# A hybrid encoder block on one core: x loaded before the first modulation's weights, scaled on ScalarE and GpSimd, with idle products on TensorE

## The chip, the cores and the metric

One core of a Trainium2 chip runs the whole kernel in one launch. The metric is device time in microseconds (us) of one execution, lower is better; three executions of the kernel before are shown, with their median. The engines are named as in the profile: PE is TensorE, DVE is VectorE, ACT is ScalarE, POOL is GpSimd, SP is the queue that issues most transfers.

## The reference

One encoder layer on 512 tokens of width 1024. Only its head is touched by the change:

```python
c_act = silu(c)
mod = c_act @ w_ada + b_ada
shift1, scale1, gate1, shift2, scale2, gate2 = split(mod, 6)
h = rmsnorm(x, g_norm1) * (1 + scale1) + shift1
z = h @ w_in
y_attn = mla_group(z[:, :448], ...)
y_sg = sgu_group(z[:, 448:], ...)
x = x + gate1 * (concat(rmsnorm(y_attn), rmsnorm(y_sg)) @ w_o)
h2 = rmsnorm(x, g_norm2) * (1 + scale2) + shift2
out = rmsnorm(x + gate2 * peer(h2), g_final)
```

`w_ada` is 1024 x 6144 in float32, so each of the six modulation vectors needs 4 MB of weights. The rest (latent attention, the gating group, the 16384 experts of `peer`) is the same before and after.

## The kernel before, in words

**The modulation vectors.** A vector of `mod` is made without TensorE doing the reduction over rows: the weights of group g come as eight tiles of 128 x 1024 (`mod_load`, L128), and VectorE adds them up, each scaled by its column of `silu(c)`, in one 128 x 1024 accumulator `macc` (`mod_group`, L138: one scaling, six fused multiply-adds, and the last one in two halves). Then eight 128 x 128 transposes on TensorE and two sums on VectorE turn the accumulator into columns (`mod_cols`, L153). There is one accumulator buffer for all groups (`tag="macc"`, L139): the next group's first write waits until the last reader of this group's sum is done. Groups 1 (scale1) and 0 (shift1) are made first, their 16 tiles loaded on SP's queue into a pool of 12 buffers; groups 2 to 5 follow later, loaded on GpSimd's queue into three buffers, behind a small copy called `mark` (L247, L373).

**The first normalization.** `normed_T` (L191) squares and sums the four 128 x 1024 blocks of x on ScalarE (L183), takes the power -1/2 on GpSimd (L114), scales x on VectorE (L197), transposes it on TensorE (L201), applies scale1 and shift1 (`affine`, L185: even columns j on VectorE, odd ones on ScalarE), and splits the result into a high and a low float32r part (`split_into`, L76: a cast on ScalarE, a subtraction on VectorE), the tiles hT.

**What follows.** `load_w` (L208) loads and splits w_in; the first product with it gives the latents `lat` and the rope key `krp` (L304 to L315). Meanwhile VectorE makes the rope angles `ang` (L272 to L281) and adds up group 2. The latents are squared, normalized (L320 to L327) and transposed (`trl`, L331); the rope key is rotated (`rope_from`, L288, with `kr_sw` on TensorE, `kr_t` and `kr` on VectorE); then the queries `qr` and `qn`, the keys `kn` and the values `v` are multiplied (L333 to L351), and the `vp` projection with `wv` follows (L372). `kr_sw` and the three `trl` share two PSUM buffers (L125).

**What sets the order.** Each engine works through its own queue in order. A scheduler sets that order when the program is built, so a change in one part can move instructions of others; SP's and GpSimd's transfers are issued in order too. From 100 us on the program is TensorE's: attention, the output projection, the routing, and the dense and gathered experts.

Lines 237 to 249 set the head:

```python
ws1 = [mod_load(1, c) for c in range(KD)]
...
    nc.sync.dma_start(t, a["x"][b * P:(b + 1) * P, :])
...
ws0 = [mod_load(0, c) for c in range(KD)]
s1 = mod_scale(1, g1c, ws1)
sh1 = mod_cols(0, ws0)
mark = nc.gpsimd.tensor_copy(mark, sh1[:, 0:1])
...
normed_T(xs, s1, sh1, hT[0], hT[1], "n1")
```

Of the kernel before, what the change touches and what calls it, by code (L numbers as in the profile page):

```python
# [9 lines left out]
F32 = mybir.dt.float32  # L10
# [5 lines left out]
ALU = mybir.AluOpType  # L16
# [41 lines left out]
def tile_kernel(ctx: ExitStack, tc: tile.TileContext, a: dict, out: bass.AP):  # L58
# [59 lines left out]
    with ExitStack() as fr:  # L118
# [34 lines left out]
        def mod_cols(g, ws=None):  # L153
            acc = mod_group(g, ws)
            m = cp.tile([P, KD], F32, name=f"mcolb{g}")
            for hf in range(2):
                p = ps.tile([P, 512], F32, name=f"mcol{g}_{hf}", tag="oacc" if ws and hf else "mod", bufs=1)
                for j in range(4):
                    nc.tensor.transpose(p[:, j * P:(j + 1) * P],  # L159
                                        acc[:, (hf * 4 + j) * P:(hf * 4 + j + 1) * P], ident)  # L160
                nc.vector.reduce_sum(m[:, hf * 4:hf * 4 + 4], p.rearrange("p (j k) -> p j k", k=P), axis=AX.X)
            nc.vector.tensor_add(m, m, bada[:, g * KD:(g + 1) * KD])
            return m

# [15 lines left out]
        def sumsq(src, dst, name):  # L180
            w = src.shape[-1]
            sq = B.tile([P, D], BF16, name=name, tag="sq", bufs=1)
            nc.scalar.activation(sq[:, :w], src, AF.Square, accum_out=dst)  # L183
# [4 lines left out]
            else:  # L188
                nc.vector.tensor_scalar(t, p, scol[:, j:j + 1], shcol[:, j:j + 1], op0=ALU.mult, op1=ALU.add)

        def normed_T(src, scol, shcol, dhi, dlo, tag, post=None):  # L191
            ss = cp.tile([P, NB], F32, name=f"ss_{tag}")
            for b in range(NB):
                sumsq(src[b], ss[:, b:b + 1], f"sq_{tag}{b}")
            r = rstd_of(ss, D, tag)
            for b in range(NB):
                nc.vector.tensor_scalar_mul(src[b], src[b], r[:, b:b + 1])  # L197
            for j in range(KD):
                p = (tr_ps if j % 3 == 2 else acc_ps)(f"trx_{tag}{j}")
                for b in range(NB):  # L200
                    nc.tensor.transpose(p[:, b * P:(b + 1) * P], src[b][:, j * P:(j + 1) * P], ident)  # L201
                t = B.tile([P, T], F32, name=f"nt_{tag}{j}", tag="nt", bufs=2)
                affine(j, t, p, scol, shcol)
                split_into(dhi[:, j, :], dlo[:, j, :], t)
                if post is not None:
                    post(j, t)

        def load_w(name, src, c0, w):  # L208
            res = []
            for kh in range(2):  # L210
                raw = B.tile([P, 4, 512], F32, name=f"{name}{kh}r", tag="wr", bufs=2)
# [2 lines left out]
                    src[kh * 512:(kh + 1) * 512, c0:c0 + w].rearrange("(c p) n -> p c n", p=P))  # L214
                hi = B.tile([P, 4, 512], F32R, name=f"{name}{kh}h", tag="wh", bufs=2)
                lo = B.tile([P, 4, 512], F32R, name=f"{name}{kh}l", tag="wl", bufs=2)
                split_into(hi[:, :, :w], lo[:, :, :w], raw[:, :, :w])
                res.append((hi, lo))
            return res

# [13 lines left out]

        m0_st = ExitStack()
        M0 = pool(m0_st, "M0", side="right")
        ws1 = [mod_load(1, c) for c in range(KD)]
        xs = []
        for b in range(NB):
            t = B.tile([P, D], F32, name=f"x{b}", tag=f"y{b}")  # L240
            nc.sync.dma_start(t, a["x"][b * P:(b + 1) * P, :])
            xs.append(t)
        ws0 = [mod_load(0, c) for c in range(KD)]
        s1 = mod_scale(1, g1c, ws1)
        sh1 = mod_cols(0, ws0)
        mark = cp.tile([P, 1], F32, name="mark")
        mark = nc.gpsimd.tensor_copy(mark, sh1[:, 0:1])  # L247
        hT = [B.tile([P, KD, T], F32R, name=f"hT{i}", tag=f"hT{i}") for i in range(2)]
        normed_T(xs, s1, sh1, hT[0], hT[1], "n1")

        m0_st.close()
        qkv_st = ExitStack()
# [7 lines left out]
        with ExitStack() as s1st:  # L260
# [35 lines left out]
                nc.vector.tensor_add(o, o, t)  # L296


            wl = load_w("wl", a["w_in"], 0, 512)
            nc.sync.dma_start(wuq, a["w_uq"].rearrange("(c p) n -> p c n", p=P))  # L300
            nc.sync.dma_start(wukv, a["w_ukv"])
            pss = [acc_ps(f"lat{b}") for b in range(NB)]
# [712 lines left out]
```

## Time and profile before

| what | value |
|---|---|
| three executions | 1567.84, 1566.68, 1567.22 us, median 1567.22 us |
| the profiled execution | 1570.06 us, of which its span is 1568.3 us |
| PE busy | 1492.6 us, 95% of the span |
| DVE busy | 1240.9 us, 79% |
| ACT busy | 636.6 us, 41% |
| POOL busy | 397.1 us, 25% |

The profile is of one execution, with the start and end of every instruction. "Idle before" is the time that an engine stood still before an instruction, with the one that ended the wait. A float32 product that is no transpose stands in the trace as two entries. The granted clock is TensorE's: 1.00 is 2.4 GHz and 0.50 is 1.2 GHz. The profiled execution took 2.84 us more than the median of the three.

### The profile page before, as it was taken

How to read it: one execution, taken by the hardware profiler on the slowest of the kernel's cores; microseconds unless marked ns; L12 is line 12 of the kernel's file. 1: busy time of each engine (PE TensorE's matmuls, PEld its weight loads, DVE VectorE, ACT ScalarE, POOL GpSimd, SP SyncE). 2: the span in 40 equal slices, each digit the busy share in tenths (PEclk: the TensorE clock that was granted, in tenths of full speed). 3: DMA queues.
4: the chain of work that ended last, by engine and by line, in shares of the span. 5: the costliest groups of instructions: out<-in, count | busy, mean ns of one | idle time of the engine just before them, and what ended most of it. 6: DMA issues, size and time to landing. Idle time of an engine off the chain costs nothing.

```text
span 1568.3 us, 21451 instructions
## 1 busy us (share of the span) xinstructions
PE 1492.6 (95%) x7675; PEld 1317.9 (84%) x7675; DVE 1240.9 (79%) x2388; ACT 636.6 (41%) x1092; POOL 397.1 (25%) x335
## 2 busy tenths in 40 slices
PE   2899999998979999999999999999999999999996
PEld 1765787887879999999999999999999999998884
DVE  6937865579989997987887878878888888886774
ACT  2533434432338997334333333333333333332343
POOL 1202100000000000002554444444544544542210
PEclk9899999999999999999999999999999999999998
DMA  9626334331325769666999999988999998987873
GB/s 366 232 79 223 130 132 148 112 104 48 101 94 159 237 211 300 218 224 220 354 351 319 321 330 328 326 318 318 336 330 314 326 325 315 333 287 230 256 237 121
DMA packets 147226, 380.71 MB, mean 243 GB/s; under 512 B 11184, under 2 KB 59840, under 8 KB 146864
## 3 DMA queue, kind: packets, MB, share of 16 engines
q1 hardware_dynamic: 103472, 221.02, 40.5%
q0 software_dynamic: 42352, 153.62, 28.7%
q10 hardware_dynamic: 1296, 4.72, 0.8%
q8 instruction: 60, 0.98, 0.2%
q14 instruction: 46, 0.38, 0.1%
HBM read 349.16 MB, written 30.15 MB: 242 GB/s over the span
## 4 chain that ended last, share of the span: by engine, by line
PE 86%; DVE 7%; DMA 3%; ACT 1%; issue 1%; POOL 0%; SPq 0%; ACTq 0%; POOLq 0%; DVEq 0%
PE out L83 11%; PE out L84 11%; PE out L82 11%; PE pa L82 11%; PE pa L84 11%; PE pa L83 11%; PE gg L770 5%; DMA wada<-w_ada 2%; PE q L82 1%; PE q L84 1%; PE q L83 1%; PE yo L82 1%; PE yo L84 1%; PE yo L83 1%; DVE macc L149 1%
## 5 line engine op out<-in xcount | busy, mean ns | idle before, releaser
L842 POOL DMA_INDIRECT gu<-peer_u,idx x128 | 181.3, 1417 | 653.6 <-DVE w17l L78 467.6
L842 POOL DMA_INDIRECT gv<-peer_v,idx x128 | 173.0, 1351 | 235.0 <-DVE accg L862 209.0
L850 DVE SCALAR_TENSOR_TENSOR scr<-gu,h2g 128x1024 bf16<-128x1024 f32 x128 | 156.5, 1222 | 24.1 <-DMA gu<-peer_u,idx 21.8
L862 DVE SCALAR_TENSOR_TENSOR accg<-gv,wg,accg 128x1024 f32<-128x1024 f32 x127 | 162.8, 1282 | 7.1 <-DMA gv<-peer_v,idx 4.6
L770 PE MATMUL gg<-o,o 128*128 128x128 f32 x768 | 96.0, 280 | 3.6 <-ACT o L764 2.0
L770 PEld LDWEIGHTS gg<-o,o 128*128 128x128 f32 x768 | 94.6, 196 | 4.1 <-ACT o L764 4.1
L908 DVE TENSOR_TENSOR a<-a,g 128x384 f32<-128x384 f32 x128 | 69.1, 550 | 6.4 <-DMA g<-gd 2.9
L764 ACT ACTIVATE o<-o1b,gT 128x128 f32<-128x128 bf16 x192 | 63.4, 405 | 13.8 <-DVE o1b L751 7.2
L518 ACT ACTIVATE a<-pa 128x384 f32<-128x384 f32 x128 | 61.7, 483 | 13.2 <-PE pa L84 13.2
L149 DVE SCALAR_TENSOR_TENSOR macc<-wada,csil,macc 128x1024 f32<-128x1024 f32 x40 | 51.2, 1280 | 9.5 <-DMA wada<-w_ada 9.1
L753 DVE TENSOR_TENSOR o<-iota_s,gT 128x1024 f32<-128x1024 f32 x48 | 58.4, 1216 | 0.3 <-PE gg L770 0.2
L757 DVE TENSOR_SCALAR o<-iota_s,gT 128x128 f32<-128x128 f32 x192 | 53.2, 339 | 0.0
L779 ACT COPY st<-gg 128x512 f32<-128x512 f32 x96 | 50.5, 581 | 0.0
L159 PE MATMUL mcol<-ident_s,macc 128*128 128x128 f32 x32 | 7.4, 391 | 26.6 <-DVE macc L146 23.1
L135 POOL DMA_DIRECT2D wada<-w_ada x32 | 17.1, 535 | 59.9 <-DVE macc L149 24.3
L159 PEld LDWEIGHTS mcol<-ident_s,macc 128*128 128x128 f32 x32 | 5.5, 201 | 28.3 <-DVE macc L146 17.9
L424 ACT ACTIVATE pe<-s,mx 128x512 f32<-128x512 f32 x16 | 11.0, 688 | 28.4 <-DVE mx L422 20.8
L684 PE MATMUL sc<-keys_s,qT 128*128 128x128 f32 x128 | 18.1, 284 | 2.8 <-ACT qT L681 2.8
L751 DVE TENSOR_TENSOR o1b<-erep,gB 128x512 bf16<-128x512 bf16 x48 | 20.0, 416 | 0.9 <-ACT gB L734 0.9
L684 PEld LDWEIGHTS sc<-keys_s,qT 128*128 128x128 f32 x128 | 15.6, 191 | 5.7 <-ACT qT L681 4.3
L531 DVE MAX8 v12d<-s 128x8 f32<-128x128 f32 x48 | 12.7, 280 | 9.4 <-ACT s L686 9.4
L431 PEld LDWEIGHTS o<-vv,pts 128*128 128x128 f32 x128 | 16.1, 192 | 2.3 <-DVE mx L422 0.8
(2789 smaller groups left out, 4952.2 us busy)
## 6 DMA issues: line engine op xcount, KB each, us to landing
gd<-st SPq DMA_DIRECT2D x12, 1984.0 KB, 7.9
g<-gd SPq DMA_DIRECT2D x31, 768.0 KB, 8.4
wada<-w_ada POOLq DMA_DIRECT2D x32, 512.0 KB, 4.7
wada<-w_ada SPq DMA_DIRECT2D x16, 512.0 KB, 10.1
x<-x SPq DMA_DIRECT2D x4, 512.0 KB, 12.4
x<-x ACTq DMA_DIRECT2D x4, 512.0 KB, 3.8
x2d<-x ACTq DMA_DIRECT2D x4, 512.0 KB, 2.8
gu<-peer_u,idx POOLq DMA_INDIRECT x128, 7.3
```

Of the source, the lines that this page charges most:

```text
L82: nc.tensor.matmul(o, lhsT=lh, rhs=rh, start=first, stop=False)
L83: nc.tensor.matmul(o, lhsT=lh, rhs=rl, start=False, stop=False)
L84: nc.tensor.matmul(o, lhsT=ll, rhs=rh, start=False, stop=last)
L149: nc.vector.scalar_tensor_tensor(acc, w, csil[:, c:c + 1], acc, op0=ALU.mult, op1=ALU.add)
L518: nc.scalar.activation(t, p[:, :TD], AF.Gelu)
L753: nc.vector.tensor_tensor(o2s[n], iota.unsqueeze(1).to_broadcast([P, UT, P]), tT[:, 1, t0:t0 + UT].unsqueeze(2).to_broadcast([P, UT, P]), ...
L764: nc.scalar.activation(o1s[n][:, i, :], e[:, :, i], AF.Copy, scale=tT[:, 2, t0 + i:t0 + i + 1])
L770: nc.tensor.matmul(pgs[n][i // 4][:, i % 4 * P:(i % 4 + 1) * P], lhsT=o2[:, i, :], rhs=o1[:, i, :], start=True, stop=True)
L842: nc.gpsimd.indirect_dma_start(out=g, out_offset=None, in_=src, in_offset=bass.IndirectOffsetOnAxis(ap=idx[:, s:s + 1], axis=0))
L850: nc.vector.scalar_tensor_tensor(scr, g, 1.0, st["h2g"], op0=ALU.mult, op1=ALU.mult, accum_out=actg[:, n:n + 1])
L862: nc.vector.scalar_tensor_tensor(accg, g, wg[:, s:s + 1], accg, op0=ALU.mult, op1=ALU.add)
L908: nc.vector.tensor_tensor(wv3, wv3, gt[:, :, e % GE, :], op=ALU.mult)
```

## The change

x's four tiles are loaded ahead of the 16 modulation tiles. Each block of x gets its own sum of squares; GpSimd does the multiply-add and the power, ScalarE the scaling, all of it ahead of the two modulation sums in the program's text, so VectorE's queue holds no scaling of x any more. After the transposes of group 1 come 24 products of the identity with the first 128 columns of the accumulator, into a PSUM buffer that nothing reads. `mark`, behind which groups 2 to 5 are loaded, now waits for the low part of column 5 of hT instead of for shift1. The split of the second half of the first w_in block is put behind the low part of column 1. `normed_T` is called from one place, so its unused `post` goes.

```diff
--- before.py
+++ after.py
@@ -159,6 +159,10 @@
                     nc.tensor.transpose(p[:, j * P:(j + 1) * P],
                                         acc[:, (hf * 4 + j) * P:(hf * 4 + j + 1) * P], ident)
                 nc.vector.reduce_sum(m[:, hf * 4:hf * 4 + 4], p.rearrange("p (j k) -> p j k", k=P), axis=AX.X)
+            if ws and g:
+                p = acc_ps("warm")
+                for k in range(24):
+                    nc.tensor.matmul(p[:, :P], lhsT=ident, rhs=acc[:, :P], start=True, stop=True)
             nc.vector.tensor_add(m, m, bada[:, g * KD:(g + 1) * KD])
             return m
 
@@ -188,13 +192,8 @@
             else:
                 nc.vector.tensor_scalar(t, p, scol[:, j:j + 1], shcol[:, j:j + 1], op0=ALU.mult, op1=ALU.add)
 
-        def normed_T(src, scol, shcol, dhi, dlo, tag, post=None):
-            ss = cp.tile([P, NB], F32, name=f"ss_{tag}")
-            for b in range(NB):
-                sumsq(src[b], ss[:, b:b + 1], f"sq_{tag}{b}")
-            r = rstd_of(ss, D, tag)
-            for b in range(NB):
-                nc.vector.tensor_scalar_mul(src[b], src[b], r[:, b:b + 1])
+        def normed_T(src, scol, shcol, dhi, dlo, tag):
+            los = []
             for j in range(KD):
                 p = (tr_ps if j % 3 == 2 else acc_ps)(f"trx_{tag}{j}")
                 for b in range(NB):
@@ -202,10 +201,10 @@
                 t = B.tile([P, T], F32, name=f"nt_{tag}{j}", tag="nt", bufs=2)
                 affine(j, t, p, scol, shcol)
                 split_into(dhi[:, j, :], dlo[:, j, :], t)
-                if post is not None:
-                    post(j, t)
-
-        def load_w(name, src, c0, w):
+                los.append(last_lo[0])
+            return los
+
+        def load_w(name, src, c0, w, after=None):
             res = []
             for kh in range(2):
                 raw = B.tile([P, 4, 512], F32, name=f"{name}{kh}r", tag="wr", bufs=2)
@@ -214,7 +213,10 @@
                     src[kh * 512:(kh + 1) * 512, c0:c0 + w].rearrange("(c p) n -> p c n", p=P))
                 hi = B.tile([P, 4, 512], F32R, name=f"{name}{kh}h", tag="wh", bufs=2)
                 lo = B.tile([P, 4, 512], F32R, name=f"{name}{kh}l", tag="wl", bufs=2)
-                split_into(hi[:, :, :w], lo[:, :, :w], raw[:, :, :w])
+                with ExitStack() as order:
+                    if after and kh:
+                        order.enter_context(tc.issue_after(after.ins))
+                    split_into(hi[:, :, :w], lo[:, :, :w], raw[:, :, :w])
                 res.append((hi, lo))
             return res
 
@@ -234,19 +236,25 @@
 
         m0_st = ExitStack()
         M0 = pool(m0_st, "M0", side="right")
-        ws1 = [mod_load(1, c) for c in range(KD)]
         xs = []
         for b in range(NB):
             t = B.tile([P, D], F32, name=f"x{b}", tag=f"y{b}")
             nc.sync.dma_start(t, a["x"][b * P:(b + 1) * P, :])
             xs.append(t)
+        ws1 = [mod_load(1, c) for c in range(KD)]
         ws0 = [mod_load(0, c) for c in range(KD)]
+        for b in range(NB):
+            ss = cp.tile([P, 1], F32, name=f"ss_n{b}")
+            sumsq(xs[b], ss, f"sq_n{b}")
+            nc.gpsimd.tensor_scalar(ss, ss, 1.0 / D, EPS, op0=ALU.mult, op1=ALU.add)
+            nc.gpsimd.tensor_tensor(ss, ss, nhalf[:, :1], op=ALU.pow)
+            nc.scalar.activation(xs[b], xs[b], AF.Copy, scale=ss)
         s1 = mod_scale(1, g1c, ws1)
         sh1 = mod_cols(0, ws0)
+        hT = [B.tile([P, KD, T], F32R, name=f"hT{i}", tag=f"hT{i}") for i in range(2)]
+        los = normed_T(xs, s1, sh1, hT[0], hT[1], "n1")
         mark = cp.tile([P, 1], F32, name="mark")
-        mark = nc.gpsimd.tensor_copy(mark, sh1[:, 0:1])
-        hT = [B.tile([P, KD, T], F32R, name=f"hT{i}", tag=f"hT{i}") for i in range(2)]
-        normed_T(xs, s1, sh1, hT[0], hT[1], "n1")
+        mark = nc.gpsimd.tensor_copy(mark, hT[1][:, 5, 0:1].bitcast(F32))
 
         m0_st.close()
         qkv_st = ExitStack()
@@ -296,7 +304,7 @@
                 nc.vector.tensor_add(o, o, t)
 
 
-            wl = load_w("wl", a["w_in"], 0, 512)
+            wl = load_w("wl", a["w_in"], 0, 512, los[1])
             nc.sync.dma_start(wuq, a["w_uq"].rearrange("(c p) n -> p c n", p=P))
             nc.sync.dma_start(wukv, a["w_ukv"])
             pss = [acc_ps(f"lat{b}") for b in range(NB)]
```

The scheduler's order changes in these places. Ahead of the latents, VectorE's queue (macc is the accumulator, wada a weight tile, x a block of x, n_r the power). Before, with what each row waits for:

```order
L167 SCALAR_TENSOR_TENSOR mcolb_150<-mcolb_150,g1c 128x8 [waits DMASW3_49,DVE_49]
L112 TENSOR_SCALAR n_ms<-ss_n_193 128x4 [waits Activation_49]
L197 TENSOR_SCALAR x_116<-x_116,n_r 128x1024 [waits DMAHW1_49,Pool_49]
L143 TENSOR_SCALAR macc_165<-wada_0_124,csil 128x1024 [waits DMAHW5_49]
L197 TENSOR_SCALAR x_118<-x_118,n_r 128x1024 [waits DMAHW2_49]
L149 SCALAR_TENSOR_TENSOR macc_165<-wada_1_126,csil,macc_165 128x1024 [waits DMAHW6_49,DVE_49]
```

And with the change, from the same place to the end of the second sum:

```order
L171 SCALAR_TENSOR_TENSOR mcolb_174<-mcolb_174,g1c 128x8 [waits DMASW3_49,DVE_49]
L143 TENSOR_SCALAR macc_214<-wada_0_124,csil 128x1024 [waits DMAHW5_49,PE_49]
L149 SCALAR_TENSOR_TENSOR macc_214<-wada_1_126,csil,macc_214 128x1024 [waits DMAHW6_49,DVE_49]
L149 SCALAR_TENSOR_TENSOR macc_214<-wada_2_128,csil,macc_214 128x1024 [waits DMAHW7_49,DVE_49]
L149 SCALAR_TENSOR_TENSOR macc_214<-wada_3_130,csil,macc_214 128x1024 [waits DMAHW0_49,DVE_49]
L149 SCALAR_TENSOR_TENSOR macc_214<-wada_4_132,csil,macc_214 128x1024 [waits DMAHW1_49,DVE_49]
L149 SCALAR_TENSOR_TENSOR macc_214<-wada_5_134,csil,macc_214 128x1024 [waits DMAHW2_49,DVE_49]
L149 SCALAR_TENSOR_TENSOR macc_214<-wada_6_136,csil,macc_214 128x1024 [waits DMAHW3_49,DVE_49]
L146 SCALAR_TENSOR_TENSOR macc_214<-wada_7_138,csil,macc_214 128x512 [waits DMAHW4_49,DVE_49]
L146 SCALAR_TENSOR_TENSOR macc_214<-wada_7_138,csil,macc_214 128x512
L78 TENSOR_TENSOR wl0l<-wl0r,wl0h 128x2048 [waits DMAHW5_49,Activation_49]
L161 TENSOR_REDUCE mcolb_224<-mcol_0_225 128x4 [waits PE_49]
```

The four scalings of x and their small step are gone, the first write of the second sum waits for TensorE, and the low part wl0l has moved ahead of the sums that make shift1 (it stood behind the first affine step).

TensorE's queue at the start of the changed kernel (trx are transposes of x, mcol those of the accumulator, warm the idle products):

```order
L200 MATMUL trx_n_258<-ident_s,x_106 128x128
L200 MATMUL trx_n_285<-ident_s,x_106 128x128
L159 MATMUL mcol_0_175<-ident_s,macc_164 128x128 x4
L159 MATMUL mcol_1_181<-ident_s,macc_164 128x128 x4
L165 MATMUL warm<-macc_164,ident_s 128x128 x24
L200 MATMUL trx_n_240<-ident_s,x_100 128x128
```

Before, the eight mcol transposes of group 1 were the first work of TensorE; now eight transposes of x stand ahead of them and the 24 products behind them, ahead of the other transposes of x.

VectorE's queue at the end of the latents (rq_ms and rkv_ms open the normalization, L326 and L327, now L334 and L335, are the scaling, kr_t and kr the rotated key). Before:

```order
L326 TENSOR_SCALAR lat<-lat,rq_r 128x256
L327 TENSOR_SCALAR lat<-lat,rkv_r 128x128
L149 SCALAR_TENSOR_TENSOR macc_734<-wada_5_750,csil,macc_734 128x1024
L149 SCALAR_TENSOR_TENSOR macc_734<-wada_6_753,csil,macc_734 128x1024
L295 TENSOR_TENSOR kr<-kr_raw,cos 128x512
L294 TENSOR_TENSOR kr_t<-kr_sw,sin 128x512
L78 TENSOR_TENSOR wv1l<-wv1r,wv1h 128x2048
```

With the change:

```order
L112 TENSOR_SCALAR rkv_ms<-lss 128x4
L149 SCALAR_TENSOR_TENSOR macc_766<-wada_5_782,csil,macc_766 128x1024
L78 TENSOR_TENSOR wv1l<-wv1r,wv1h 128x2048
L302 TENSOR_TENSOR kr_t<-kr_sw,sin 128x512
L303 TENSOR_TENSOR kr<-kr_raw,cos 128x512
L334 TENSOR_SCALAR lat<-lat,rq_r 128x256
L304 TENSOR_TENSOR kr<-kr,kr_t 128x512
L335 TENSOR_SCALAR lat<-lat,rkv_r 128x128
```

The low part wv1l and one more step of the key have moved ahead of the scaling of the latents. All six steps of group 2 up to wada_5 now stand between the last part of hT and this place; before, the first two stood ahead of hT's end. Behind the values v the order of every engine is the one of before.

## Rows read from the trace of the kernel before

**Rows 1.** The page: its first line.
```profile
span 1568.3 us, 21451 instructions
```

**Rows 2.** A stretch: length, PE, PEld, DVE, ACT, POOL busy, clock, DMA share, GB/s.
```profile
90.00:100.00 10.00, 10.00 (x35) 6.27 (x34) 3.04 (x4) 3.51 (x6) 1.04 (x2) 1.00 0.14 53
```

**Rows 3.** Timeline, VectorE, 5 to 37 us: start, length, line, tiles, idle before.
```profile
5.28 0.75 DVE L143 TENSOR_SCALAR macc<-wada,csil 128x1024 f32<-128x1024 f32 x1 [5.28 <-DMA wada<-w_ada]
...
17.12 1.41 DVE L146 SCALAR_TENSOR_TENSOR macc<-wada,csil,macc 128x512 f32<-128x512 f32 x2
...
25.31 0.75 DVE L143 TENSOR_SCALAR macc<-wada,csil 128x1024 f32<-128x1024 f32 x1
25.98 0.74 DVE L197 TENSOR_SCALAR x<-x,n_r 128x1024 f32<-128x1024 f32 x1
...
30.36 5.24 DVE L149 SCALAR_TENSOR_TENSOR macc<-wada,csil,macc 128x1024 f32<-128x1024 f32 x4
...
35.63 1.42 DVE L146 SCALAR_TENSOR_TENSOR macc<-wada,csil,macc 128x512 f32<-128x512 f32 x2
```

**Rows 4.** Timeline, ScalarE: the last square of x.
```profile
22.07 1.06 ACT L183 ACTIVATE sq_n<-x 128x1024 bf16<-128x1024 f32 x1 [0.15 <-DMA x<-x]
```

**Rows 5.** Timeline, TensorE, 17 to 39 us: transposes.
```profile
17.92 1.97 PE L159 MATMUL mcol<-ident_s,macc 128*128 128x128 f32 x8 [17.92 <-DVE macc L146]
...
28.64 1.34 PE L201 MATMUL trx_n<-ident_s,x 128*128 128x128 f32 x6 [0.32 <-DVE x L197]
30.49 0.88 PE L201 MATMUL trx_n<-ident_s,x 128*128 128x128 f32 x6 [0.52 <-DVE x L197]
...
36.53 1.94 PE L159 MATMUL mcol<-ident_s,macc 128*128 128x128 f32 x8 [5.16 <-DVE macc L146]
```

**Rows 6.** Timeline, TensorE: four 128x128 float32 products, two entries each.
```profile
128.44 1.05 PE L431 MATMUL o<-vv,pts 128*128 128x128 f32 x8
```

**Rows 7.** Three stretches, columns as in 2: the granted clock.
```profile
18.00:20.00 2.00, 1.89 (x8) 1.49 (x8) 1.29 (x3) 1.62 (x3) 0.00 (x0) 1.00 1.03 420
36.00:38.00 2.00, 1.47 (x7) 1.50 (x8) 1.39 (x3) 0.58 (x1) 0.00 (x0) 0.50 1.05 422
77.00:78.00 1.00, 1.00 (x3) 0.46 (x2) 0.00 (x0) 0.19 (x1) 1.00 (x3) 0.79 0.86 299
```

**Rows 8.** Timeline, VectorE, 39 to 54 us.
```profile
39.43 0.81 DVE L189 TENSOR_SCALAR nt_n<-trx_n,mcolb,mcolb 128x512 f32<-128x512 f32 x1
...
40.16 2.28 DVE L78 TENSOR_TENSOR wl0l<-wl0r,wl0h 128x2048 fp32r<-128x2048 f32 x1
...
52.46 1.28 DVE L78 TENSOR_TENSOR hT<-nt_n,hT 128x512 fp32r<-128x512 f32 x2
```

**Rows 9.** Timeline, ScalarE: an affine step and two casts.
```profile
50.72 0.78 ACT L187 ACTIVATE nt_n<-trx_n,mcolb,mcolb 128x512 f32<-128x512 f32 x1 [0.90 <-DVE hT L78]
51.53 1.14 ACT L77 CAST hT<-nt_n 128x512 fp32r<-128x512 f32 x2
```

**Rows 10.** Timeline, GpSimd: its first power, first loads; the page: DMA issue to landing.
```profile
23.58 1.03 POOL L114 TENSOR_TENSOR n_r<-n_ms,nhalf 128x4 f32<-128x4 f32 x1 [14.90 <-DVE n_ms L112]
...
39.69 1.64 POOL L135 DMA_DIRECT2D wada<-w_ada  x3
...
wada<-w_ada POOLq DMA_DIRECT2D x32, 512.0 KB, 4.7
```

**Rows 11.** Timeline, VectorE, 67 to 75 us.
```profile
67.17 0.29 DVE L327 TENSOR_SCALAR lat<-lat,rkv_r 128x128 f32<-128x128 f32 x1 [0.63 <-POOL rkv_r L114]
...
71.86 0.68 DVE L294 TENSOR_TENSOR kr_t<-kr_sw,sin 128x512 f32<-128x512 f32 x1
72.46 2.28 DVE L78 TENSOR_TENSOR wv1l<-wv1r,wv1h 128x2048 fp32r<-128x2048 f32 x1
```

**Rows 12.** Timeline, TensorE: last latent transposes, first query products.
```profile
72.60 1.97 PE L331 MATMUL trl<-ident_s,lat 128*128 128x128 f32 x8 [1.63 <-DVE kr_t L294]
74.36 4.26 PE L336 MATMUL qr<-cT_s,wuq_s 128*128 128x512 f32 x6
```

## The prediction

> **What bounds the kernel now.** First I read the page: the span is 1568.3 us [rows 1]; the profiled execution of 1570.06 us has 1.76 us around it and lies 2.84 us above the median of 1567.22 us. So I work out a difference on this trace and add it to the median. Then the stretches: from about 74 us on TensorE is hardly ever idle, as in 90 to 100 us, where it is busy for 10.00 of 10.00 us [rows 2], and behind the values v the change leaves every queue in its old order. Whatever the head gains or loses up to the first query product, at 74.36 us [rows 12], therefore moves the end by as much. Third, the timeline of the head. Up to 37 us VectorE sums two sets of modulation weights. The first sum starts when its first tile lands, at 5.28 us, and ends at 18.53 us; the second starts at 25.31 us, with three of the four scalings of x (0.74 us) between its steps, and ends at 37.05 us [rows 3]. After that VectorE has hardly a gap: shift1 is ready at 39.43 us, the last low part of hT ends at 53.74 us [rows 8], and kr_t, for which TensorE waits with the last latent transposes, at 72.54 us [rows 11, 12]. So this is a VectorE chain with TensorE's transposes in it, and the question is what the change does to that chain.
>
> **Step 1: x goes first.** The transfers land one behind the other, 512 KB each: eight tiles of the first sum, then four of x. The last of x, the twelfth, is there at 22.07 us [rows 4]. With the change the twelfth is the last weight tile of the first sum. Its two halves take 1.41 us [rows 3], so that sum ends at 23.5 instead of 18.53 us, 5.0 us later. The transposes end 1.36 us behind it (17.92 + 1.97 against 18.53 [rows 3, 5]), at 24.9 us. ScalarE's squares and scalings (eight of about 1.06 us [rows 4]) follow x's four tiles, which land in the places of the first four weight tiles, and end at about 17 us; GpSimd's eight small steps lie among them.
>
> **Step 2: the 24 idle products.** They read the one accumulator, and the order shows the second sum's first write waiting for TensorE, so the second sum starts when the last product is done. Four such products take 1.05 us at the full clock [rows 6]; without the last one's run-out of some 0.17 us that is 0.22 us each, 0.44 us at half. Which clock? The stretch 18 to 20 us shows 1.00, that of 36 to 38 us 0.50 [rows 7], yet eight transposes take 1.97 us in the one and 1.94 us in the other [rows 5]. I go by the durations: half. Six transposes take 1.34 us at 28.64 us and 0.88 us at 30.49 us [rows 5], so the rate rose about there, 4 to 5 us behind the first of these transposes, which followed the scaling that began at 24.6 us, ahead of the second sum [rows 3]; the rise in the stretch 77 to 78 us comes about 5 us after TensorE had begun again at 72.6 us [rows 7, 12]. Here work begins at 22.9 us, so I put the rise at 27.9 us: 3.0 us of products at half (7 of them), 17 at 0.22 us, the last one's run-out, and the second sum starts at 31.9 us. At the full clock throughout, the transposes ending 0.9 us earlier, it would be 29.5 us; at half throughout, 35.6 us.
>
> Transposes of x were all that TensorE did in the five us ahead of the faster six at 30.49 us [rows 5]. The Trainium skill ("TensorE: Matmul & The Clock Gate", Part 4) says the opposite, that a transpose doesn't count as work for the clock in the same way; by it the rise would come about 2 us later, the products would end 1 us later, and the sum would be 7.7 us instead of 6.7. I go by the row.
>
> **Step 3: the second sum alone.** 0.75 us, six steps of 1.31 (5.24 us for four) and 1.42 us make 10.0 us [rows 3]: 31.9 to 41.9 us, 4.9 us later than now. The scalings that leave VectorE are worth 3 x 0.67 us between the steps, one more ahead of them and the wait for GpSimd's power; they are in this difference.
>
> **Step 4: up to hT.** wl0l, 2.2 us [rows 8], now comes ahead of the sums that make shift1 and hides the transposes; with 1.6 us for these sums the first affine step starts at 45.7 instead of 39.43 us. From there to the last low part it took 14.3 us. Taken out are wl0l (2.2) and the first two steps of group 2 (1.9, by 0.75 and 1.28 less overlap). But those two and wl0l covered a wait: ScalarE's affine step and cast, 0.78 + 0.57 us [rows 9], are longer than VectorE's own affine step of 0.8, so three of the four pairs of columns now wait some 0.65 us. That gives 12.2 us, so 57.9 instead of 53.74 us: 4.2 us later.
>
> **Step 5: up to the query products.** Between the last part of hT and kr_t lay 18.8 us. Added ahead of the scaling of the latents: the split wv1l, 2.2 us, and the last step of the key, 0.6 us [rows 11]; the first step of group 2, 0.7 us; and a wait for its tile. `mark` now follows the low part of column 5, at about 54.7 us, the loads go out at 54.9 us instead of 39.69 and land 4.7 us later [rows 10], at 59.6 us, where VectorE wants the first at 58.3: 1.3 us. Saved are the waits for GpSimd, 0.63 us for the longest [rows 11] and about 1.3 us in all. So 22.3 us, and the last scaling ends at 80.2 us. Two transposes, ScalarE's copy and four more transposes take as long as the eight transposes do now, 1.9 us; the query products start at 82.1 us, 7.7 us later.
>
> **Step 6: the clock there.** Now the query products run at half from 74.4 to 77.5 us. In the changed kernel the transposes start about 2 us ahead of the last scaling, at 78.3, so the rise is due at about 83.3 us and only 1.2 us run at half: half the difference, 1.0 us, comes back.
>
> **Sum:** 7.7 - 1.0 = 6.7 us on the trace (1576.8 us for that execution). The estimates of steps 4 and 5 lean to the long side, so I take 6.3 us: **1573.5 us** for the median. Nothing later takes it up: the tiles of the next group are loaded during the query products and wanted only behind the vp projection.
>
> **Rivals.** A difference of 0.2%, 3.1 us, is about what a measurement of this kernel can tell from none.
>
> - *The clock holds* (not slower). If the products run at the full clock and it stays there from 29 us to the queries, step 2 gives 2.4 us back, and TensorE's half-rate stretch at 74.4 to 77.5 us (1.5 us), the transposes ahead of it (1.0) and around shift1 (0.3) go. 6.3 - 5.2 is about 1 us: 1568.4 us, no change. It decides if the clock is full when the products start. Against it: eight transposes at half in the same place [rows 5], and TensorE has nothing to do from about 34 us (its other transposes done) until the second sum's end at 41.9 us. Chance 0.13.
> - *Faster.* For that the second sum would have to start before about 25 us, that is, not to wait for the products, the change not doing what its order says: 5.9 us come back, and 1.0 us more if the tile of group 2 is not waited for. That is 1566.6 us, not yet beyond 0.2%; it needs a further 2.5 us of absorbed waits in the attention stage. Chance 0.06, and 0.04 for something in between that ends within 0.2%.
> - *Half all the way.* The products never lift the clock: the second sum starts 3.7 us later, 1577.2 us. Chance 0.10.
> - *x is late.* TensorE has eight transposes of x ahead of those of the accumulator, and they want x scaled by 22.9 us. By ScalarE's rows the fourth block is ready at about 17 us. GpSimd's first use of its power function may cost a start-up that the trace of before can hide in 14.9 us of idle time [rows 10]; if it takes all of these, the fourth block is ready at about 29 us and all moves by 6 us: 1579.5 us. Chance 0.05. The Trainium skill ("SBUF — State Buffer", "Who interferes with whom") says that a GpSimd instruction that reads SBUF and a VectorE one with two SBUF inputs shut each other out, and here they now overlap; by it each of four powers could wait for one sum step of 1.28 us, x would be ready at 22 us, and TensorE would still not wait. No row before shows such an overlap.
>
> **How the numbers follow.** The forecast has 0.62, all of it slower by over 0.2%. Slower: 0.62 + 0.10 + 0.05 = 0.77; same: 0.13 + 0.04 = 0.17; faster: 0.06. The range must leave out no more than 0.2: it starts at 1566.5 us, which leaves out the faster cases, and ends at 1578.0 us, beyond half all the way, leaving out most of the late x.
>
> **What would show it.** In the changed trace: the first sum ends at 23 to 24 us; VectorE then stands still for about 5 us, released by TensorE's product; the second sum ends at about 42 us; the last part of hT near 58 us; VectorE waits about 1 us for a tile of group 2; the first query product starts at about 82 us; from 100 us on everything is as before, moved by 6 us. I am wrong if the second sum ends before 39 us, or if the query products start before 79 us, or if the difference at 116 us is not that at the end.

## The result, and the profile after

The changed kernel took 1576.3 us (median of six executions, 1575.78 to 1581.07) against 1567.5 us for the kernel before in the same session: a ratio of 1.0063, with a 95% interval of 1.0052 to 1.0075. That is slower by 8.2 to 11.8 us. One of the six executions of the kernel before took 7608.3 us and does not count in the ratio. The forecast was 1573.5 us in a range of 1566.5 to 1578.0 us.

The profiled execution took 1575.92 us; the first line of its page answers to [rows 1].

```profile
span 1574.1 us, 21548 instructions
```

VectorE's timeline of the changed kernel, the columns as in [rows 3], which it answers together with [rows 8, 11]:

```profile
11.33 0.75 DVE L143 TENSOR_SCALAR macc<-wada,csil 128x1024 f32<-128x1024 f32 x1 [11.33 <-DMA wada<-w_ada]
...
22.43 1.42 DVE L146 SCALAR_TENSOR_TENSOR macc<-wada,csil,macc 128x512 f32<-128x512 f32 x2
...
26.16 0.17 DVE L171 SCALAR_TENSOR_TENSOR mcolb<-mcolb,g1c 128x8 f32<-128x8 f32 x1
31.30 0.75 DVE L143 TENSOR_SCALAR macc<-wada,csil 128x1024 f32<-128x1024 f32 x1 [4.97 <-PE warm L165]
...
40.01 1.42 DVE L146 SCALAR_TENSOR_TENSOR macc<-wada,csil,macc 128x512 f32<-128x512 f32 x2
41.34 2.28 DVE L78 TENSOR_TENSOR wl0l<-wl0r,wl0h 128x2048 fp32r<-128x2048 f32 x1
...
45.06 0.81 DVE L193 TENSOR_SCALAR nt_n<-trx_n,mcolb,mcolb 128x512 f32<-128x512 f32 x1
46.58 1.29 DVE L78 TENSOR_TENSOR hT<-nt_n,hT 128x512 fp32r<-128x512 f32 x2 [0.71 <-ACT hT L77]
...
56.42 1.29 DVE L78 TENSOR_TENSOR hT<-nt_n,hT 128x512 fp32r<-128x512 f32 x2 [0.84 <-ACT hT L77]
...
59.27 0.75 DVE L143 TENSOR_SCALAR macc<-wada,csil 128x1024 f32<-128x1024 f32 x1 [1.22 <-DMA wada<-w_ada]
...
79.28 0.28 DVE L335 TENSOR_SCALAR lat<-lat,rkv_r 128x128 f32<-128x128 f32 x1
```

The row at 31.30 us is the result in short: scale1 is ready at 26.33 us, and VectorE stands still for 4.97 us until TensorE has read the accumulator for the last time. TensorE's timeline, which answers to [rows 5, 12], has the other side of it:

```profile
23.23 1.97 PE L159 MATMUL mcol<-ident_s,macc 128*128 128x128 f32 x8 [6.07 <-DVE macc L146]
24.99 6.27 PE L165 MATMUL warm<-macc,ident_s 128*128 128x128 f32 x48
...
40.82 1.97 PE L159 MATMUL mcol<-ident_s,macc 128*128 128x128 f32 x8 [7.81 <-DVE macc L146]
...
77.44 0.69 PE L339 MATMUL trl<-ident_s,lat 128*128 128x128 f32 x2 [1.92 <-DVE lat L334]
78.49 1.61 PE L339 MATMUL trl<-ident_s,lat 128*128 128x128 f32 x6 [0.37 <-DVE lat L334]
80.66 1.12 PE L339 MATMUL trl<-ident_s,lat 128*128 128x128 f32 x4 [0.56 <-ACT cT_s L340]
81.57 4.23 PE L344 MATMUL qr<-cT_s,wuq_s 128*128 128x512 f32 x6
```

The 24 products (48 entries) take 6.27 us, and the query products start at 81.57 instead of 74.36 us [rows 12], 7.2 us later. From there nothing is made up for a long time: v starts at 98.7 instead of 91.5 us, the first product of group 2's row (`mrow`) at 123.9 instead of 116.7 us, the last of the 768 products `gg` starts at 614.3 instead of 607.2 us, and the first of `out` at 623.8 instead of 616.6 us. The spans differ by 5.8 us only: what follows took 1.4 us less in this execution than in that of before. It goes bit by bit among the products of `out`, of which the last starts at 1558.6 instead of 1553.0 us.

### The profile page after: what moved, and what is told of

Same layout as the page of the kernel before. It is cut to its first block, busy times and chain, and to the rows that moved or that the text cites. A ratio compares the mean times of both kernels' runs of the same rounds, so it can differ in the third digit from the quotient of the medians.

```text
span 1574.1 us, 21548 instructions
## 1 busy us (share of the span) xinstructions
PE 1497.8 (95%) x7723; PEld 1322.3 (84%) x7723; DVE 1238.3 (79%) x2383; ACT 640.5 (41%) x1096; POOL 405.6 (26%) x342
## 4 chain that ended last, share of the span: by engine, by line
PE 85%; DVE 9%; DMA 3%; issue 2%; ACT 1%; SPq 0%; POOL 0%; POOLq 0%; ACTq 0%; DVEq 0%
PE out L82 11%; PE out L84 11%; PE out L83 11%; PE pa L82 11%; PE pa L84 11%; PE pa L83 11%; PE gg L778 5%; DMA wada<-w_ada 3%; DVE macc L149 1%; PE q L82 1%; PE q L83 1%; PE q L84 1%; PE yo L82 1%; PE yo L84 1%; PE yo L83 1%
## 5 line engine op out<-in xcount | busy, mean ns | idle before, releaser
L200 PE MATMUL trx_n<-ident_s,x 128*128 128x128 f32 x32 | 6.6, 354 | 17.6 <-ACT x L251 14.4
L432 ACT ACTIVATE pe<-s,mx 128x512 f32<-128x512 f32 x16 | 11.0, 688 | 29.3 <-DVE mx L430 21.5
L200 PEld LDWEIGHTS trx_n<-ident_s,x 128*128 128x128 f32 x32 | 4.5, 177 | 19.2 <-ACT x L251 15.6
```

## The experiments

Executions of one kernel differ by up to 5.5 us (the kernel before: 1565.2 to 1570.7 us in one set), so a single span says little, and the medians of two sets are not compared directly. The table has three measures for each kernel: where the first query product and the first product of v start in its trace (one execution), and the ratio to the kernel before run beside it, with its 95% interval, also as microseconds on 1567.5 us.

| kernel | qr starts | v starts | ratio (interval) | us |
|---|---|---|---|---|
| before | 74.4 | 91.5 | 1 | 0 |
| the change | 81.6 | 98.7 | 1.0063 (1.0052 to 1.0075) | +9.9 |
| no_warm: without products | 75.9 | 92.3 | 1.0019 (1.0010 to 1.0028) | +3.0 |
| two_acc: products, two accumulators | 75.0 | 92.4 | 1.0003 (0.9994 to 1.0012) | +0.5 |
| warm48: 48 products | 87.9 | 104.4 | 1.0085 (1.0071 to 1.0099) | +13.3 |
| warm_ident: products of the identity | 76.5 | 94.0 | 1.0011 (1.0002 to 1.0020) | +1.7 |
| before_warm: before, with products | 75.7 | 92.7 | 1.0007 (0.9998 to 1.0016) | +1.1 |
| w_first_no_warm: no products, weights first | 74.6 | 92.1 | 1.0001 (0.9992 to 1.0010) | +0.2 |
| old_mark: the change, mark behind shift1 | 84.7 | 100.9 | 1.0076 (1.0062 to 1.0090) | +11.9 |
| no_warm_old_mark: no products, mark behind shift1 | 73.2 | 90.1 | 0.9980 (0.9971 to 0.9990) | -3.1 |
| w_first_no_warm_old_mark: only x's scaling moved | 71.8 | 89.0 | 0.9978 (0.9969 to 0.9987) | -3.4 |
| best_x: no products, two accumulators, mark behind shift1 | 70.3 | 85.9 | 0.9975 (0.9966 to 0.9984) | -3.9 |

### The products taken away (no_warm)

```diff
-            if ws and g:
-                p = acc_ps("warm")
-                for k in range(24):
-                    nc.tensor.matmul(p[:, :P], lhsT=ident, rhs=acc[:, :P], start=True, stop=True)
```

> The change without the 24 idle products. Theory (the wait): the second sum no longer waits for TensorE's products, so it starts at about 26.0 us, right behind the two sums over the transposes (24.39 to 25.93 us in the changed kernel), instead of 31.30 us, and ends at about 36.2 instead of 41.43 us; the low part wl0l falls behind the first affine step again; the query products start 5 to 6 us earlier, at 75.5 to 76.5 us, and the median is 5 to 6 us below the changed kernel, about 1570.5 us, still 2 to 4 us above the kernel before. Rival 1 (load order): x first is what costs, the products lie beside it; the query products start at 80 us or later and the median stays above 1574.5 us. Rival 2 (clock): the products pay by their clock; without them TensorE's half-rate stretch grows and gives back 2 us or more, so the median is 1572.5 us or more although the second sum starts at 26 us.

VectorE's timeline without the products:

```profile
24.59 0.69 DVE L161 TENSOR_REDUCE mcolb<-mcol 128x4 f32<-128x512 f32 x1 [0.16 <-PE mcol L159]
25.20 0.74 DVE L143 TENSOR_SCALAR macc<-wada,csil 128x1024 f32<-128x1024 f32 x1
...
33.90 1.42 DVE L146 SCALAR_TENSOR_TENSOR macc<-wada,csil,macc 128x512 f32<-128x512 f32 x2
```

The second sum follows the transposes' sums at once, 6.1 us earlier, and the query products start 5.7 us earlier. The ratio falls from 1.0063 to 1.0019. So the products are the largest part of the cost, and rivals 1 and 2 are out.

### The same products, but no wait (two_acc)

```diff
-            acc = B.tile([P, D], F32, name=f"macc{g}", tag="macc")
+            acc = (M0 if ws and g else B).tile([P, D], F32, name=f"macc{g}", tag="macc", bufs=1)
```

> The change with all 24 products in their place, but the sums of the first two groups each have an accumulator of their own. Theory (the wait): TensorE does the same work, and only the wait is gone; the second sum starts at about 23.9 us, at once behind the first, and ends at 34 to 36 us (the last weight tiles may be what it waits for); the query products start at 74 to 75.5 us, and the median is 1567 to 1570 us, 6.5 to 9 us below the changed kernel. Rival 1 (load order): above 1574.5 us. Rival 2 (the products hold up TensorE's own work, so that what stands behind them on TensorE is late): the transposes of x and of the second sum are late by 5 us in turn, the first affine step starts after 41 us, and the median is above 1572 us.

TensorE's timeline with two accumulators:

```profile
21.31 1.97 PE L159 MATMUL mcol<-ident_s,macc 128*128 128x128 f32 x8 [3.94 <-DVE macc L146]
23.07 6.07 PE L165 MATMUL warm<-macc,ident_s 128*128 128x128 f32 x48
28.98 1.91 PE L200 MATMUL trx_n<-ident_s,x 128*128 128x128 f32 x16
33.19 1.32 PE L159 MATMUL mcol<-ident_s,macc 128*128 128x128 f32 x8 [2.30 <-DVE macc L146]
```

And VectorE's, of the same kernel:

```profile
22.60 0.75 DVE L143 TENSOR_SCALAR macc<-wada,csil 128x1024 f32<-128x1024 f32 x1 [0.68 <-DMA wada<-w_ada]
...
32.38 1.42 DVE L146 SCALAR_TENSOR_TENSOR macc<-wada,csil,macc 128x512 f32<-128x512 f32 x2
```

The products take about as long as in the change (6.07 against 6.27 us), now beside the second sum, and the kernel is not told apart from the one before: 1.0003. So it is not the work on TensorE that costs, but who waits for the buffer that it reads. The second buffer gives something besides: the second sum starts at 22.60 us, ahead even of the 25.20 us of no_warm, since it no longer waits for the transposes of the first sum either. Here the products even give something: the eight transposes of the second sum take 1.32 us, where they took 1.97 us in the change. That 0.65 us is all that was seen of the products' use, and it needs the second sum to end soon after them.

### Twice as many (warm48)

```diff
-                for k in range(24):
+                for k in range(48):
```

> The change with 48 products instead of 24. Theory (the wait): 24 more products at the full clock, 0.22 us each, make the second sum start 5.3 us later, at 36.6 us, and the query products 5.3 us later, at 86.9 us; the median is about 1581.5 us. Rival 2 (clock): TensorE stays busy until about 36.5 us, the clock is held longer, and a part of 1 to 3 us comes back: 1578.5 to 1580.5 us.

VectorE's timeline with 48 products:

```profile
37.34 0.75 DVE L143 TENSOR_SCALAR macc<-wada,csil 128x1024 f32<-128x1024 f32 x1 [11.23 <-PE warm L165]
```

The wait grows from 4.97 to 11.23 us. The query products start 6.3 us later than in the change instead of 5.3 us: with 48 products the row takes 12.53 us, 6.26 us more than the 6.27 us of the change. That is not a slower product: TensorE's rate rose later here. Stretches of this kernel, columns as in [rows 2]:

```profile
26.00:28.00 2.00, 2.00 (x12) 2.00 (x11) 0.12 (x1) 0.00 (x0) 0.00 (x0) 1.00 1.04 414
28.00:30.00 2.00, 2.00 (x19) 2.00 (x18) 0.00 (x0) 0.00 (x0) 0.00 (x0) 1.00 1.02 408
```

The change has 18 entries in 26 to 28 us (below), this kernel 12: its rate rises at about 28.3 us instead of 26.6 us, so 8 products run at half and not 4. At the full rate an entry follows the other after 0.11 us in both, the 0.22 us a product of [rows 6]. The median was 1581.83 us, near the 1581.5 us of the theory; by the ratios the 24 products more cost only 3.4 us, with intervals that overlap.

### Products that wait for nothing (warm_ident)

```diff
-                    nc.tensor.matmul(p[:, :P], lhsT=ident, rhs=acc[:, :P], start=True, stop=True)
+                    nc.tensor.matmul(p[:, :P], lhsT=ident, rhs=ident, start=True, stop=True)
```

> The change with its 24 products multiplying the identity with itself instead of with the accumulator, so nothing on VectorE waits for them (they go to the front of TensorE's queue). Theory (the wait): as without products, the query products start at 75.5 to 76.5 us, median 1569.5 to 1572 us. Rival 2 (clock): early products lift the clock for the transposes and the latents and bring 1 us or more against the kernel without products (1570.9 us): below 1569.5 us. Rival (TensorE is held up): the transposes of the first sum, queued behind the products, are late, above 1572.5 us.

The products run from 5.58 us on. Stretches of this kernel, columns as in [rows 2]:

```profile
10.00:12.00 2.00, 2.00 (x20) 2.00 (x20) 0.03 (x1) 1.15 (x2) 0.70 (x3) 1.00 1.02 399
...
16.00:18.00 2.00, 1.93 (x9) 1.82 (x10) 1.96 (x2) 1.05 (x2) 0.00 (x0) 0.50 1.03 422
```

Their rate doubles by 10 to 12 us, but at 16 to 18 us the granted clock is 0.50 again, and the eight transposes of the first sum, at 23.37 us, take 1.97 us as in the change. The ratio, 1.0011, is not told apart from the 1.0019 of no_warm, and the query products start no earlier (76.5 against 75.9 us): no use of an early lift of the clock is seen here.

### The kernel before with the products alone (before_warm)

The four lines of no_warm's diff, added to the kernel before.

> The kernel before with nothing but the 24 products added. Theory (the wait, which costs only what reaches past other work): the products run from about 20 us, 7 at half and 17 at the full clock, to about 27 us. VectorE has two scalings of x ahead of the second sum's first write there and would reach it at about 26.0 us, so only about 1 us is lost: median 1568 to 1570 us. If the products run at half throughout, to 30.5 us, it is 4.5 us: 1572 us. Rival 1 (the products cost their whole length wherever they stand): 1573 us or more. Rival 2 (clock): no loss or a gain, below 1567 us.

VectorE's timeline of the kernel before with the products:

```profile
24.60 1.42 DVE L201 TENSOR_SCALAR x<-x,n_r 128x1024 f32<-128x1024 f32 x2 [1.23 <-POOL n_r L114]
27.34 0.75 DVE L143 TENSOR_SCALAR macc<-wada,csil 128x1024 f32<-128x1024 f32 x1 [1.33 <-PE warm L165]
```

Here the same products take 7.50 us and cost about 1 us (1.0007; no change is inside the interval): they begin at 19.81 us, while VectorE is waiting for x and scaling it, and only the last 1.33 us reach past that cover. In the change x comes first and its scaling has left VectorE, so the cover is gone. The price of the products is made by the other parts of the change.

### The load order (w_first_no_warm)

```diff
+        ws1 = [mod_load(1, c) for c in range(KD)]
         xs = []
...
-        ws1 = [mod_load(1, c) for c in range(KD)]
```

This and the lines of no_warm's diff.

> The change without the products and with the weight tiles of the first sum loaded ahead of x again; ScalarE and GpSimd still scale x, mark is still late. Theory: the first sum ends at 18.5 us, the second starts when its first tile, the thirteenth, lands, at about 23.5 us, and goes at the pace of the tiles (about 1.45 us each), so it ends at 35 us, only 1.2 us ahead of the kernel without products alone: the load order is worth 1 to 1.5 us, median about 1569.3 us. Rival 1 (load order): worth 4 to 6 us, 5 us being the delay of the first sum; the median is 1564.5 to 1566.5 us.

VectorE's timeline with the weights first and no products:

```profile
16.95 1.41 DVE L146 SCALAR_TENSOR_TENSOR macc<-wada,csil,macc 128x512 f32<-128x512 f32 x2
...
23.27 0.75 DVE L143 TENSOR_SCALAR macc<-wada,csil 128x1024 f32<-128x1024 f32 x1 [2.41 <-DMA wada<-w_ada]
...
32.56 1.41 DVE L146 SCALAR_TENSOR_TENSOR macc<-wada,csil,macc 128x512 f32<-128x512 f32 x2
```

The first sum ends 5.0 us earlier than with x first (23.33 us in no_warm), but the second one only 1.35 us earlier (33.97 against 35.32 us): its tiles come behind x, and VectorE waits 2.41 us for the first. That is 1.3 us at the query products, 0.3 us at v, 2.8 us by the ratios: between nothing and 3 us, and less than the first sum's delay. With mark behind shift1 (below) it is 1.4, 1.1 and 0.3 us.

### Mark behind shift1 (old_mark, w_first_no_warm_old_mark, no_warm_old_mark)

```diff
         sh1 = mod_cols(0, ws0)
+        mark = cp.tile([P, 1], F32, name="mark")
+        mark = nc.gpsimd.tensor_copy(mark, sh1[:, 0:1])
...
-        mark = cp.tile([P, 1], F32, name="mark")
-        mark = nc.gpsimd.tensor_copy(mark, hT[1][:, 5, 0:1].bitcast(F32))
...
-            wl = load_w("wl", a["w_in"], 0, 512, los[1])
+            wl = load_w("wl", a["w_in"], 0, 512)
```

First in the change as it is:

> The change with its products and with x first, but mark behind shift1 as in the kernel before and the split of w_in's second half not put behind the low part of column 1. Theory: from the last low part of hT to the first query product the changed kernel takes 23.9 us against 20.6 us before, because of a tile wait of 1.2 us, the split wv1l and steps of the key and of group 2 ahead of the scaling of the latents; this order takes back 1 to 3 us: the query products start at 78.5 to 80.5 us, median 1573.3 to 1575.3 us. Rival (all of the cost lies ahead of shift1): the order is worth nothing, the median stays at 1575.8 to 1576.8 us.

This was a miss: 1.0076, not faster than the change; v starts 2.2 us later in its trace. VectorE's timeline of old_mark:

```profile
32.65 0.75 DVE L143 TENSOR_SCALAR macc<-wada,csil 128x1024 f32<-128x1024 f32 x1 [6.24 <-PE warm L165]
...
51.22 0.80 DVE L193 TENSOR_SCALAR nt_n<-trx_n,mcolb,mcolb 128x512 f32<-128x512 f32 x1
56.02 0.75 DVE L143 TENSOR_SCALAR macc<-wada,csil 128x1024 f32<-128x1024 f32 x1 [4.00 <-DMA wada<-w_ada]
```

TensorE's, of the same kernel:

```profile
25.07 7.54 PE L165 MATMUL warm<-macc,ident_s 128*128 128x128 f32 x48
```

And GpSimd's:

```profile
48.52 0.18 POOL L255 COPY mark<-mcolb 128x1 f32<-128x1 f32 x1 [33.62 <-DVE mcolb L166]
48.75 1.67 POOL L135 DMA_DIRECT2D wada<-w_ada  x3
```

Of the 2.2 us at v, 1.35 us lie ahead of mark: the same 24 products take 7.54 us here instead of 6.27 us, since the rate rises only at about 29.3 us, and the second sum starts at 32.65 instead of 31.30 us. The intervals of the two ratios overlap, so that old_mark is the slower one is not shown; only that the gain of 1 to 3 us is not there.

And the edit is not mark alone. Without `los[1]` one split of w_in (wl1l) stands ahead of shift1, and the first step of group 2 comes behind only one pair of hT's columns: VectorE gets there 3.5 us after mark's start, the tile lands 7.3 us after its issue, and the rest of hT waits 4.00 us. With mark behind shift1 and `los[1]` kept, the scheduler puts wl1l behind the second affine step and the first step of group 2 behind two pairs of columns, as in the kernels below; that program was not timed. So this run does not tell what mark alone is worth with the products in place. Without them:

> The kernel before with one part of the change only: x is scaled by ScalarE and GpSimd; weights first, no products, mark behind shift1. Theory: the first affine step starts at about 36.4 us as without the products and with the weights first, 3 us ahead of the kernel before, and the order behind it no longer gives these back (there the query products started at 74.6 us in spite of it): they start at 71 to 72 us, median 1564.5 to 1566 us, faster than the kernel before by 2 to 3 us. Rival (VectorE's scalings of x are hidden by the wait for weight tiles): no gain, 1567 us or more.

> x first and scaled by ScalarE and GpSimd, no products, one accumulator, mark behind shift1. Theory: what the late mark costs does not depend on the load order, so against the kernel without products (1570.9 us, query products at 75.9 us) this gains about as much as with the weights first (1569.0 to 1563.4 us): the query products start at 72.5 to 73.5 us, median 1565 to 1567 us, and against the kernel with the weights first and mark behind shift1 (1563.4 us) the load order costs 1 to 2.5 us. Rival: with x first, the second sum ends later and the first loads of group 2 collide with it, so that mark behind shift1 gains under 1.5 us: 1569.5 us or more.

VectorE's timeline of w_first_no_warm_old_mark:

```profile
36.80 0.81 DVE L189 TENSOR_SCALAR nt_n<-trx_n,mcolb,mcolb 128x512 f32<-128x512 f32 x1
...
45.78 0.74 DVE L143 TENSOR_SCALAR macc<-wada,csil 128x1024 f32<-128x1024 f32 x1
```

Here mark is copied at 36.83 us and the first step of group 2 stands 9 us behind it, so it waits for nothing and fills the gap that VectorE would stand idle for ScalarE's cast. Both kernels gain: 1.0001 to 0.9978 and 1.0019 to 0.9980, or 3.6 and 6.1 us; in the traces the query products start 2.8 and 2.7 us earlier. The second gain was larger by the ratio than the 5.6 us that the medians of two sets had led me to expect, and smaller by the trace. In these two kernels, unlike in old_mark, keeping the `los[1]` gives the same order of instructions on every engine, so here it is mark that counts.

The first of these kernels is the kernel before with one thing changed, x's scaling on ScalarE and GpSimd. It is faster than before by 2.0 to 4.9 us (its median of 1563.43 us is 1 us below what was expected): that part of the change is good by itself.

### What beats both (best_x)

x first, the second accumulator of two_acc, mark behind shift1, no products.

> x first, scaled by ScalarE and GpSimd, no products, two accumulators, mark behind shift1. Theory: the second sum follows the first with hardly a wait and the first affine step starts at about 35.5 us; the low part wl0l then waits about 1.8 us for ScalarE's cast, so hT ends about where it does with the weights first; the query products start at 71 to 72 us, median 1564.5 to 1566 us. Rival (load order): the later first sum costs against the kernel with the weights first and old mark, 1567 us or more.

It took 0.9975 of the kernel before (0.9966 to 0.9984), 2.5 to 5.3 us less, and is not told apart from w_first_no_warm_old_mark. In its trace the query products start earliest of all. TensorE's timeline of best_x:

```profile
70.28 2.74 PE L340 MATMUL qr<-cT_s,wuq_s 128*128 128x512 f32 x6
```

The six entries take 2.74 us here against 4.26 us before [rows 12]: in this execution the clock was up when they began.

## Why the prediction was right in sign, and where it was off

Step by step, forecast and trace:

- **x first:** the first sum ends at 23.85 us (forecast 23.5), and x is scaled at 16.4 us (about 17), as ScalarE's timeline of the changed kernel shows:

```profile
12.15 4.27 ACT L251 ACTIVATE x<-x,ss_n 128x1024 f32<-128x1024 f32 x4 [1.21 <-POOL ss_n L250]
```

- **The products:** the second sum starts at 31.30 us (forecast 31.9). The rise of the rate, put at 27.9 us, came at about 26.6 us, so 4 products ran at half and 20 at the full rate, not 7 and 17; stretches of the changed kernel, columns as in [rows 2], show it by their entries, 11 at half, 21 at the full rate, and already 18 in 26 to 28 us:

```profile
24.00:26.00 2.00, 2.00 (x11) 2.00 (x10) 1.42 (x3) 0.00 (x0) 0.00 (x0) 1.00 1.03 410
26.00:28.00 2.00, 2.00 (x18) 2.00 (x17) 0.30 (x2) 0.00 (x0) 0.00 (x0) 1.00 1.03 410
28.00:30.00 2.00, 2.00 (x21) 2.00 (x20) 0.00 (x0) 0.00 (x0) 0.00 (x0) 1.00 1.03 410
...
38.00:40.00 2.00, 0.00 (x0) 0.00 (x0) 1.94 (x2) 1.73 (x1) 0.00 (x0) 0.50 0.77 304
...
82.00:84.00 2.00, 2.00 (x3) 0.67 (x2) 0.07 (x1) 0.50 (x1) 1.59 (x3) 0.50 0.75 203
84.00:86.00 2.00, 2.00 (x5) 0.83 (x4) 0.40 (x1) 0.58 (x1) 0.00 (x0) 0.86 0.78 264
```

  The 5 us from the start of TensorE's work to the rise was the weak term of step 2. The transposes of the first sum begin at 23.23 us in the change, 23.02 us in warm48 and 23.31 us in old_mark, and the rise comes at about 26.6, 28.3 and 29.3 us. With the rise of old_mark the forecast would have been short by 0.8 us, with this one it was long by 0.6 us; that it came out so near is in part luck.
- **The second sum** takes 10.1 us (forecast 10.0) and ends at 41.43 us.
- **Up to hT:** the first affine step starts at 45.06 us (forecast 45.7), the three waits for ScalarE are 0.71, 0.84 and 0.84 us (forecast 0.65 each), and the last low part ends at 57.71 us (forecast 57.9).
- **Up to the queries:** the wait for group 2's tile is 1.22 us (forecast 1.3), the last scaling ends at 79.56 us (80.2), and the query products start at 81.57 us (82.1).
- **The clock at the queries, step 6, failed.** It was to give back 1.0 us. The rise came at 84.6 us, in the last of these stretches, not at 83.3, and the six entries take 4.23 us, as long as the 4.26 us before [rows 12]. The transposes had begun at 77.44 us, 7.1 us ahead of the rise, where the forecast took 5 us. They were spread by waits, which the forecast left out; that the waits put the rise off is not shown. With 0 in place of 1.0, and the 7.2 us that was measured where 7.7 had been summed, the head costs 7.2 us.

So the cost that the forecast put at 6.3 us is 7.2 us in the head of the trace. The ratio's interval begins at 8.2 us. The remaining 1 us or more was not found in any stage: between the traces the shift stays at 7.1 to 7.4 us up to `out` and is 5.8 us at the end. That is by 1.4 us not the difference at 116 us, which the prediction had named as a sign of being wrong, and what takes it back in `out` is not explained. A part lies in which executions were met: two of the six, at 1580.92 and 1581.07 us, stand over 4.6 us above the other four, of which the traced one is one; the medians alone differ by 8.8 us, and the traced execution of before stands some 2.5 us above its median. In the other kernels the ratio and the start of the queries differ by up to 1.9 us in either direction, so one execution doesn't settle it; it stays open.

Of the rivals, "the clock holds" fell at 38 to 40 us (granted clock 0.50, TensorE idle), "half all the way" with the entries above, "x is late" with ScalarE's row. "Faster", that the second sum would not wait for the products, is what two_acc builds, and even that was only level with the kernel before. It still has the late mark and the products; best_x, without both, is faster, but which of the two counts there was not taken apart.

Taken apart by the start of the query products, from the kernel before in four steps: scaling moved off VectorE 74.4 to 71.8 us (-2.6), mark late to 74.6 (+2.8), x first to 75.9 (+1.3), products to 81.6 us (+5.7). By the ratios the four are -3.4, +3.6, +2.8 and +6.9 us. The prediction had the sum almost right, but hid a gain of some 3 us inside step 3 and a loss as large inside steps 4 and 5. The sizes belong to this sequence: what an early mark alone would give with the products in, no run shows, since old_mark drops `los[1]` too.

## What to carry to other kernels

Idle work that is to keep an engine running is a reader of the buffer that it multiplies: give it data that nobody wants to overwrite, or a second buffer, and ask who writes next. Price it by what of it reaches past other waits, not by its length: the same 24 products cost about 1 us in one order of loads and 6 us in another. Where a scheduler fixes the order of use, the moment at which loads are released has to be fitted to that order: releasing them early was worth some 3 to 6 us where the order of use stayed, and nothing that was seen where the same edit also moved a split and the first use forward. And when a step takes the time of the clock's rise from a trace, give it a range: among three kernels that start alike it came at 26.6, 28.3 and 29.3 us.

## What was not expected of the hardware

**GpSimd's powers beside VectorE.** The two powers ahead of the latents' scaling took 1.04 and 1.00 us before. GpSimd's timeline of the changed kernel:

```profile
11.29 2.98 POOL L250 TENSOR_TENSOR ss_n<-ss_n,nhalf 128x1 f32<-128x1 f32 x4
...
72.71 1.86 POOL L114 TENSOR_TENSOR rq_r<-rq_ms,nhalf 128x4 f32<-128x4 f32 x1
74.56 2.18 POOL L114 TENSOR_TENSOR rkv_r<-rkv_ms,nhalf 128x4 f32<-128x4 f32 x1
```

VectorE runs a step of group 2 and the split wv1l at that time, each with two inputs from SBUF; before, it ran short steps and copies. The pair was 1.86 and 2.19 us in no_warm, where the same two stand beside it, and 1.03 and 1.00 us in best_x, where they don't. The Trainium skill ("SBUF — State Buffer", "Who interferes with whom") says that such a VectorE instruction contends with a GpSimd one that reads SBUF; the direction agrees. No wait for GpSimd stands ahead of the scaling here, since steps of the key come in between, so it cost nothing that the trace shows. The four powers of x's sums of squares, beside the first sum, took 2.98 us in the change, 3.71 us in no_warm and 3.99 us in best_x; x was scaled by 16.4 us in the change all the same, so they did not wait for a step of the sum each, as the prediction had weighed.

**The granted clock at the start.** The stretch of 24 to 26 us shows 1.00 with 11 entries, that of 28 to 30 us 1.00 with 21, both with TensorE busy throughout. In this trace the granted clock is first recorded at 26.5 us, and ahead of that the column stands at 1.00: at the start of the program the durations tell the rate, not this column.
